# Moving low-part products, one tile offset and the start of the gathered rows in a two-layer fp32 transformer trunk

## The chip, the cores and the metric

One NeuronCore of one Trainium2 chip runs the whole program in one launch. The metric is device time in microseconds (us); lower is better. Each figure for a kernel is the median of several executions, and one execution was taken with the hardware profiler.

## The reference, cut to what matters

256 tokens of width 1024 go through two layers. Each layer is a mixer and a feed-forward part, each with a residual and a LayerNorm:

```python
for layer in range(2):
    mix = mla_mixer(h, ...) if layer == 0 else nsa_mixer(h, shared, ...)
    h = layer_norm(ALPHA * h + mix, ln_g[layer, 0], ln_b[layer, 0])
    ffn = peer_ffn(h, p_w_q[layer], p_subkeys[layer], p_u[layer], p_v[layer])
    h = layer_norm(ALPHA * h + ffn, ln_g[layer, 1], ln_b[layer, 1])
```

The feed-forward part picks 128 of 16384 experts for each token (8 heads, 16 each), and sums them with gates:

```python
u_e, v_e = u[experts], v[experts]
a = gelu(einsum("thkd,td->thk", u_e, xc))
out = einsum("thk,thkd->td", g * a, v_e)
```

All is float32.

## The kernel before, in words

**Split products.** Every weight block (128 partitions by 1024) is loaded by SyncE into a raw buffer, ScalarE casts it to a high part (`hi`, line 125, `_shi`), and VectorE subtracts to get the low part (`lo`, line 136, `_slo`). Activations are split in the same way: `hT[0]` holds the high part of the transposed hidden state and `hT[1]` the low part. A product is then three TensorE passes: high by high, low activation by high weight, high activation by low weight. Every product is issued at line 202. `hi` and `lo` have four buffers each. A high tile is allocated 32 elements longer than its contents, and `self.odd` says whether a tile begins at element 32 or 0 for every second buffer; a weight that is not in `self.odd` always begins at 0.

**Order.** Nothing reorders the program: each engine takes its instructions in the order in which the Python code issues them. `nxt()` hands out the next weight of one long list and prepares the two behind it (`prep`).

**Stages.** The order is mixer A, feed-forward 0, mixer B, feed-forward 1. A feed-forward stage does all experts instead of gathering for most tokens: (1) queries and scores, with VectorE's top-k work drained beside TensorE ("side" work); (2) the u stage, 128 steps `u_step`, one per block of 128 experts, which from the point where the routing is done works "wide" (512 columns at once, high by both parts of `hT`, then low by high); (3) the v stage, 128 steps `v_mm`, each with six products for token tile 0 and four for token tile 1. The last 64 tokens are not in the dense sums: for these VectorE adds 64 gathered tiles of `p_v` rows, one row for each partition (`g_mac`, line 493), GpSimd gathers the rows (`g_row`, line 479, a ring of `RING = 6`) and the activations that belong to them out of a DRAM scratch `actD` (`g_act`, line 483, four columns per small tile `gel`, multiplied into the gates at line 488). `actD` is written from the u stage (line 770). Row `gc` is added at the step `j` at which `j >= LEAD + int(rate * gc)` with `rate = (P - 8 - LEAD) / 64`. The low part of the next weight stands ahead of the row in VectorE's order. In the last steps weights are held in "keep" tiles so that token tile 1 can be finished behind token tile 0.

**Joints.** Between two stages the LayerNorm stands on the path: sum (line 273, or 854 and 855), statistics (276), `ln_mid` (285 to 292), `ln_center` (280) and `ln_scale` (298), then `ln_T`: four transposes on TensorE (229), a copy by ScalarE (312, high part) and a subtraction by VectorE (313, low part), which `ln_T` returns as a function to be issued later. Token tile 0 is normalised first; the work of tile 1 then runs beside early products of the next stage (`early_mm(tt, x, w, tiles)`: token tile, part of the activation, part of the weight, and which of four weights). Each such entry is a pair of products, 24 entries in all; `early_mm` leaves out those that were done, and `early_close` does the rest. `lo_aside` has GpSimd make the first low weight. Joint A leads from mixer A to feed-forward 0 and joint C from mixer B to feed-forward 1 (both through `out_close`); joint B leads from feed-forward 0 to mixer B (end of `peer`). The end of feed-forward 1 has no next stage and no transposes.

Of the kernel before, what the change touches and what calls it, by code (L numbers as in the profile page):

```python
# [34 lines left out]
FIRST, NEXT = 44, 10  # L35
GT = 64
ND = S - GT
RING, LEAD = 6, 7
AHEAD = 12
GB = 0.8  # L40
GS = 2.0 ** 15
# [2 lines left out]
class Kern:  # L44
# [276 lines left out]
    def ln_last(self, early, los=()):  # L321


        los, done = list(los), bool(los)
        if early:
            self.early_open()
            self.early_mm(0, 0, 0, (0, 1))
            self.early_mm(0, 1, 0, (0, 1))
        if not done:
            los.append(self.ln_T(0, 1))  # L330
        if early:
            self.early_mm(0, 0, 0, (2, 3))
        for hf in range(2):
            self.ln_scale(1, hf)
            if done and hf == 0:
                los.pop(0)()
            los.append(self.ln_T(1, hf))
            if done and early and hf == 0:
                self.early_mm(0, 1, 0, (2, 3))
            if early and hf == 0:  # L340
                self.early_mm(1, 0, 0, (0, 1))
        for f in los:
            f()
# [105 lines left out]
    def peer(self, l):  # L449
        tc, nc, I = self.tc, self.nc, self.I  # L450
        self.v0 = self.v0s.pop(0)
        with ExitStack() as es:
# [188 lines left out]
            done = {"g": 0, "a": 0}  # L641

            def g_flush(n=1):
                if len(gq) < n:
                    return
                while gq:
                    t0, oi, gs = gq.popleft()
                    ps = self.acc(t0 // 4 % 2)
                    for q in range(4):
                        for w in range(2):  # L650
                            self.mm(ps[:, q * P:(q + 1) * P], oi[:, q // 2, :, q % 2], gs[w][:, q // 2, :, q % 2],
                                    w == 0, w == 1)
                    pv = ps.rearrange("p (t j) -> p j t", t=4)
                    k = done["a"]
                    for x, j0, n in A:
                        m = min(max(k, 0), n)
                        if m > 0:
                            y = x[:, 0:m, t0:t0 + 4]
                            nc.vector.scalar_tensor_tensor(y, pv[:, j0:j0 + m], 1.0 / GS, y, op0=OP.mult, op1=OP.mult)  # L659
                        if m < n:  # L660
                            nc.scalar.activation(x[:, m:n, t0:t0 + 4], pv[:, j0 + m:j0 + n], AF.Copy, scale=1.0 / GS)
                        k -= n
                    done["g"] = t0 + 4
# [63 lines left out]
            def u_step(j):  # L727
                hi, lo = self.nxt()
                ps = self.ps()
                wide = len(A) > 1  # L730
                if wide:

                    def high(k):
                        self.mm(ps, hi[:, k * P:(k + 1) * P], self.hTT[:, k].rearrange("p a t -> p (a t)"), k == 0, k == KC - 1)

                    for k in range(KC - 1):
                        high(k)
                    for k in range(KC):
                        self.mm(ps[:, 0:S], lo[:, k * P:(k + 1) * P], xhi[:, k, :], False, False)
                    high(KC - 1)  # L740
                else:
                    self.proj_T(ps[:, 0:S], hi, lo, xhi, xlo, KC)
                return j, ps, wide
# [4 lines left out]
            def u_fin(x):  # L748
                while due:
                    y, ps = due.popleft()  # L750
                    nc.vector.tensor_tensor(y, y, ps, op=OP.mult)
                if x is None:
                    return
                j, ps, wide = x
                jj = (P - FIRST + j) % P
                y, n = slot(jj), done["g"]
                if wide:
                    t = gat.tile([P, S], F32, tag="half", name="half", bufs=2)
                    nc.scalar.copy(t, ps[:, S:2 * S])  # L759
                    nc.vector.tensor_tensor(ps[:, 0:S], ps[:, 0:S], t, op=OP.add)  # L760
                if n:
                    nc.scalar.activation(ps[:, 0:n], ps[:, 0:n], AF.Gelu)  # L762
                    due.append((y[:, 0:n], ps[:, 0:n]))
                if n < ND:
                    nc.scalar.activation(y[:, n:ND], ps[:, n:ND], AF.Gelu)  # L765
                if j % 4 == 0:
                    gst.append(gat.tile([P, 4, GT], F32, tag="gst", name="gst", bufs=2))
                nc.scalar.activation(gst[-1][:, j % 4, :], ps[:, ND:S], AF.Gelu)  # L768
                if j % 4 == 3:
                    nc.gpsimd.dma_start(self.actD[:, jj - 3:jj + 1, :], gst.pop())  # L770
                done["a"] = j + 1
# [24 lines left out]
            for j in range(P):  # L796
                x = u_step(j)
                u_fin(pu)
                pu = x
                g_flush(2)  # L800
                run_side(1.6 if len(A) == 1 else GB)
                if not side and len(A) == 1:
                    es_r.close()
                    if l == 1:
                        self.odd.update((i, 0) for i in range(self.si, self.v0))
                    hot = self.pr8.tile([P, 2, 3, 2, P, 2], F16, tag="r8", name="hot")
                    A.append((self.pr8.tile([P, NEXT, ND], F32, tag="r8", name="A2"), 0, NEXT))
                    n = P - FIRST - NEXT
                    A.append((pool(es_1, "slots1").tile([P, n, ND], F32, name="A1"), NEXT, n))
                    side.append(g_gen(hot))  # L810
                if done["g"] == ND and j >= P - 3 and not W:
                    w_start()
# [36 lines left out]
            def sum_1(f):  # L849

                t = self.ps()
                c, z = accs[1][f], hN[0:P - GT, 1, f * 512:(f + 1) * 512]
                nc.scalar.copy(t[0:P - GT], c[P - GT:P])
                nc.vector.scalar_tensor_tensor(z, z, ALPHA, c[0:P - GT], op0=OP.mult, op1=OP.add)
                nc.vector.tensor_tensor(z, z, t[0:P - GT], op=OP.add)
# [36 lines left out]
            early = l == 0 and "nsa" in self.parts  # L892
# [12 lines left out]
            lo0 = []  # L905
            for f in range(2):
                for j in range(P - NT, P - 3):
                    v_mm(j, 1, (f,), False, j == P - 4)
                    if f == 1 and j == P - 7:
                        lo0.append(self.ln_T(0, 1))  # L910
                sum_1(f)
                if early and f == 0:
                    self.lo_aside()
                self.ln_stats(1, f)
                if f == 0:
                    self.ln_T(0, 0)()
            self.ln_mid(1)
            self.ln_last(early, lo0)
        return hN


# [230 lines left out]
    def out_close(self):  # L1152

        two, again = (0, 1), not self.oboth
        base = self.si + 2
        if again:
            self._slo(base + 1)
            self.oacc[1] = [self.acc(1) for _ in range(2)]
            self.out_mm(4, 1, two, True, False)
        self.out_step(6)  # L1160
        if again:
            self._slo(base + 2)
        self.warm(AF.Sqrt)
        self.out_step(7)
        self.ln_start(self.ohN, self.ogb, self.oacc)
        for hf in range(2):
            self.ln_sum(0, hf)
            self.ln_stats(0, hf)
        if again:
            self.out_mm(5, 1, two, False, False)  # L1170
        if again:
            self._slo(base + 3)
        self.ln_mid(0)
        if again:
            for k in range(4):
                self.owts[k] = self.nxt(False, False)
        early = "peer1" in self.parts if again else "peer0" in self.parts
        if early:
            self._shi(self.si + 3)
        for hf in range(2):  # L1180
            self.ln_scale(0, hf)

        for k in ((6, 7, 2, 3) if again else (5, 6, 7)):
            self.out_mm(k, 1, two, False, False)
        last = (0, 1) if again else (2, 3)
        for f in range(2):
            self.out_mm(last[0], 1, (f,), False, False)
            self.out_mm(last[1], 1, (f,), False, True)
            self.ln_sum(1, f)
            if early and f == 0:  # L1190
                self.lo_aside()
            self.ln_stats(1, f)
            if f == 0:
                self.ln_T(0, 0)()
        self.ln_mid(1)
        self.ln_last(early)

    def heads_T(self, dst, h0, ps):

# [475 lines left out]
```

## Time and profile before

| what | us |
|---|---|
| median of 3 runs | 1750.76 |
| lowest and highest of these | 1747.94, 1750.95 |
| the profiled execution, its own time | 1745.92 |
| span of its records | 1744.1 |

The profiled execution is one of its own, 4.84 us below the median. The 1.8 us between its time and its span lie outside the recorded instructions. Rows give times from the start of the span. A line of a timeline begins with start and length of a run of instructions in us, then engine, line, operation, output and inputs, and in brackets how long the engine had been idle before it and which engine and line ended that wait.

### The profile page before, as it was taken

Reading aid. Unit: us, or ns where it says so; the run is one execution under the profiler, and the core shown is the slowest. Engines: PE = TensorE matmul, PEld = TensorE weight load, DVE = VectorE, ACT = ScalarE, POOL = GpSimd, SP = SyncE. Lnnn points to the kernel's source line nnn. Section 1 sums busy time; section 2 is a strip of 40 time slices with the busy share of each in tenths; the row PEclk is TensorE's granted clock in tenths of the full one; section 3 lists DMA queues with packets and bytes.
Section 4 is the critical chain, followed back from the end, with each engine's and each line's share of the span. In section 5 each row is a group of like instructions: output and inputs, shape, how many; then the busy total and the mean of one; then the engine's idle time right before and its main releaser. Section 6 shows DMA issues by size and latency. Waiting matters only on the chain.

```text
span 1744.1 us, 30698 instructions
## 1 busy us (share of the span) xinstructions
PE 1702.4 (98%) x10610; PEld 1480.5 (85%) x10610; DVE 1553.4 (89%) x3667; ACT 1041.5 (60%) x2265; POOL 478.7 (27%) x441
## 2 busy tenths in 40 slices
PE   7999999999999999999998999999999999999997
PEld 6779999888888788888786789998888888888886
DVE  6778988989997899999767789988999998999998
ACT  6656555766666455556455755556666666555554
POOL 2010002000002777761342210002000005777740
PEclk9999999999999999999998999999999999999999
DMA  7545667555557799999572265657556558999992
GB/s 245 174 145 180 203 192 266 184 183 185 183 184 259 301 395 373 368 358 328 176 246 90 84 215 179 204 182 270 187 182 188 183 183 297 401 383 369 361 363 108
DMA packets 118619, 416.66 MB, mean 239 GB/s; under 512 B 16032, under 2 KB 18112, under 8 KB 117376
## 3 DMA queue, kind: packets, MB, share of 16 engines
q1 hardware_dynamic: 88976, 322.60, 54.6%
q0 software_dynamic: 29488, 92.10, 14.2%
q8 instruction: 84, 1.38, 0.3%
q14 instruction: 71, 0.58, 0.1%
HBM read 400.49 MB, written 13.63 MB: 237 GB/s over the span
## 4 chain that ended last, share of the span: by engine, by line
PE 69%; issue 16%; DVE 7%; DMA 3%; ACT 2%; POOL 2%; SPq 0%; POOLq 0%; ACTq 0%; DVEq 0%
PE acc L202 36%; PE mm L202 33%; DVE lo L136 2%; PE mm L229 1%; DMA actD<-gst 1%; POOL row L479 1%; POOL actD L770 1%; DVE keep L136 1%; DMA raw<-a_wv 1%; ACT hi L125 0%; DMA xT<-xT 0%; DMA gel<-actD,gidx 0%; POOL gel L483 0%; DVE gacc L493 0%; DVE W L786 0%
## 5 line engine op out<-in xcount | busy, mean ns | idle before, releaser
L125 ACT CAST hi<-raw 128x1024 fp32r<-128x1024 f32 (+1 forms) x463 | 484.3, 1048 | 237.8 <-PE acc L202 96.7
L202 PE MATMUL mm<-hT,hi 128*128 128x256 f32 (+1 forms) x3360 | 610.7, 328 | 0.0
L136 DVE TENSOR_TENSOR lo<-raw,hi 128x1024 fp32r<-128x1024 f32 (+1 forms) x459 | 559.3, 1222 | 29.2 <-ACT hi L125 27.7
L202 PEld LDWEIGHTS mm<-hT,hi 128*128 128x128 f32 x3360 | 484.0, 188 | 44.0 <-issue 1.2
L202 PE MATMUL acc<-hi,W 128*128 128x512 f32 x1452 | 408.7, 390 | 0.0
L202 PEld LDWEIGHTS acc<-hi,W 128*128 128x128 f32 x1452 | 273.2, 188 | 56.9
L202 PE MATMUL mm<-hT,lo 128*128 128x256 f32 x2376 | 320.0, 277 | 0.0
L202 PEld LDWEIGHTS mm<-hT,lo 128*128 128x128 f32 x2376 | 306.9, 188 | 15.1
L202 PE MATMUL acc<-lo,W 128*128 128x512 f32 x968 | 299.6, 391 | 2.6 <-DVE lo L136 2.6
L770 POOL DMA_DIRECT2D actD<-gst x64 | 34.8, 544 | 785.0 <-ACT gst L768 785.0
L479 POOL DMA_INDIRECT row<-p_v,gidx x128 | 195.4, 1527 | 119.0 <-DVE gacc L493 81.7
L202 PEld LDWEIGHTS acc<-lo,W 128*128 128x128 f32 x968 | 181.6, 188 | 42.1 <-DVE lo L136 4.9
L125 ACT CAST hi<-spare 128x1024 fp32r<-128x1024 f32 x122 | 128.1, 1050 | 115.9 <-PE acc L202 99.8
L483 POOL DMA_INDIRECT gel<-actD,gidx x128 | 162.8, 1272 | 49.9 <-issue 36.0
L493 DVE SCALAR_TENSOR_TENSOR gacc<-row,ggate,gacc 128x1024 f32<-128x1024 f32 x126 | 161.3, 1280 | 1.1
L136 DVE TENSOR_TENSOR lo<-spare,hi 128x1024 fp32r<-128x1024 f32 x122 | 148.8, 1219 | 5.8 <-ACT hi L125 5.1
L762 ACT ACTIVATE mm<-mm 128x192 f32<-128x192 f32 (+23 forms) x170 | 40.9, 241 | 122.6 <-DVE mm L760 122.6
L786 DVE TENSOR_TENSOR W<-A,W 128x128 fp32r<-128x128 f32 (+1 forms) x512 | 107.5, 252 | 1.8 <-ACT W L781 1.8
L760 DVE TENSOR_TENSOR mm<-mm,half 128x256 f32<-128x256 f32 x174 | 74.5, 428 | 15.5 <-ACT half L759 14.9
L781 ACT CAST W<-A 128x192 fp32r<-128x192 f32 x256 | 88.2, 346 | 0.0
L659 DVE SCALAR_TENSOR_TENSOR A<-acc,A 128x176 f32<-128x176 f32 (+16 forms) x268 | 56.8, 274 | 24.9 <-PE acc L202 19.9
L765 ACT ACTIVATE A<-mm 128x192 f32<-128x192 f32 (+23 forms) x244 | 67.4, 276 | 7.2 <-DVE mm L760 2.2
(276 smaller groups left out, 1755.6 us busy)
## 6 DMA issues: line engine op xcount, KB each, us to landing
raw<-p_u SPq DMA_DIRECT2D x256, 512.0 KB, 3.8
spare<-p_v SPq DMA_DIRECT2D x64, 1024.0 KB, 8.9
raw<-p_v SPq DMA_DIRECT2D x63, 1024.0 KB, 8.9
raw<-p_wq SPq DMA_DIRECT2D x32, 512.0 KB, 4.0
actD<-gst POOLq DMA_DIRECT2D x64, 128.0 KB, 3.8
raw<-b_wo SPq DMA_DIRECT2D x12, 512.0 KB, 3.5
raw<-a_wo SPq DMA_DIRECT2D x8, 512.0 KB, 4.2
raw<-s_wT SPq DMA_DIRECT2D x8, 512.0 KB, 4.3
```

The lines of the kernel that those rows point to most:

```text
L125: self.nc.scalar.copy(self.his[i], self.raws[i])
L136: e.tensor_tensor(self.los[i], raw, self.his[i].bitcast(F32), op=OP.subtract)
L202: self.nc.tensor.matmul(out, a, b, start=start, stop=stop)
L479: nc.gpsimd.indirect_dma_start(out=t, out_offset=None, in_=gtable, in_offset=bass.IndirectOffsetOnAxis(ap=gidx[:, 0, c:c + 1], axis=0))
L483: nc.gpsimd.indirect_dma_start(out=gel[c // 4][:, c % 4:c % 4 + 1], out_offset=None, in_=gplaces, in_offset=bass.IndirectOffsetOnAxis(ap=g ...
L493: nc.vector.scalar_tensor_tensor(gacc, t, gw[:, c:c + 1], gacc, op0=OP.mult, op1=OP.add)
L659: nc.vector.scalar_tensor_tensor(y, pv[:, j0:j0 + m], 1.0 / GS, y, op0=OP.mult, op1=OP.mult)
L760: nc.vector.tensor_tensor(ps[:, 0:S], ps[:, 0:S], t, op=OP.add)
L765: nc.scalar.activation(y[:, n:ND], ps[:, n:ND], AF.Gelu)
L770: nc.gpsimd.dma_start(self.actD[:, jj - 3:jj + 1, :], gst.pop())
L781: nc.scalar.copy(WW[j][:, 0:ND], slot(j))
L786: nc.vector.tensor_tensor(WW[j][:, o:o + c.stop - c.start], slot(j)[:, c], WW[j][:, c].bitcast(F32), op=OP.subtract)
```

## The change

Four edits. (1) `LEAD` goes from 7 to 11: the first gathered row is added at step 11 of the v stage, and the rest closer together; the last stays at step 118. (2) In both layers, and not in layer 1 alone, the high parts of u's weights begin at element 32 in every second buffer once the u stage is wide. (3) In joints A and C the low part of tile 0's first half is not subtracted right after its copy but after `ln_scale(1, 0)`, and the products that read it go behind tile 1's first transposes; in joint B the low part of tile 0's second half goes from behind `ln_scale(1, 0)` to ahead of `sum_1(1)`, and the products that read it ahead of tile 1's first transposes. (4) In all three joints two products with the first low weight (`early_mm(0, 0, 1, (0,))`) go from `early_close` to ahead of tile 1's first transposes.

```diff
-RING, LEAD = 6, 7
+RING, LEAD = 6, 11
...
     def ln_last(self, early, los=()):
-        los, done = list(los), bool(los)
+        los = list(los)
         if early:
             self.early_open()
             self.early_mm(0, 0, 0, (0, 1))
+        if los:
+            los.append(self.ln_T(0, 1))
+        elif early:
             self.early_mm(0, 1, 0, (0, 1))
-        if not done:
-            los.append(self.ln_T(0, 1))
         if early:
             self.early_mm(0, 0, 0, (2, 3))
+            if not los:
+                self.early_mm(0, 1, 0, (2, 3))
+            self.early_mm(0, 0, 1, (0,))
         for hf in range(2):
             self.ln_scale(1, hf)
-            if done and hf == 0:
+            if hf == 0 and los:
                 los.pop(0)()
             los.append(self.ln_T(1, hf))
-            if done and early and hf == 0:
-                self.early_mm(0, 1, 0, (2, 3))
             if early and hf == 0:
+                self.early_mm(0, 1, 0, (0, 1))
                 self.early_mm(1, 0, 0, (0, 1))
         for f in los:
             f()
...
                     es_r.close()
-                    if l == 1:
-                        self.odd.update((i, 0) for i in range(self.si, self.v0))
+
+                    self.odd.update((i, 0) for i in range(self.sh, self.v0))
...
                     if f == 1 and j == P - 7:
                         lo0.append(self.ln_T(0, 1))
+                for x in lo0:
+                    x()
                 sum_1(f)
...
             self.ln_mid(1)
-            self.ln_last(early, lo0)
+            self.ln_last(early)
...
             self.ln_stats(1, f)
             if f == 0:
-                self.ln_T(0, 0)()
+                lo0 = self.ln_T(0, 0)
         self.ln_mid(1)
-        self.ln_last(early)
+        self.ln_last(early, [lo0])
```

## Rows read from the trace of the kernel before

**Rows 1.** The page, part 1: TensorE's busy time, share and instructions.

```profile
PE 1702.4 (98%) x10610; PEld 1480.5 (85%) x10610; DVE 1553.4 (89%) x3667; ACT 1041.5 (60%) x2265; POOL 478.7 (27%) x441
```

**Rows 2.** Windows: stretch, length, busy per engine; wide u and v, each layer.

```profile
304.81:547.34 242.53, 242.53 (x1636) 212.49 (x1634) 223.02 (x553) 160.29 (x450) 10.80 (x20) 1.00 0.57 183
1200.79:1442.40 241.61, 241.61 (x1635) 212.50 (x1633) 223.67 (x555) 160.91 (x451) 10.80 (x20) 1.00 0.58 181
547.56:836.74 289.18, 286.37 (x1254) 235.73 (x1253) 273.09 (x469) 166.48 (x261) 175.93 (x126) 0.99 0.92 346
1442.63:1727.71 285.08, 284.86 (x1254) 234.59 (x1252) 272.72 (x469) 165.06 (x258) 171.29 (x126) 1.00 0.92 345
```

**Rows 3.** Timeline, TensorE, start of the v stage of layer 0.

```profile
570.27 0.61 PE L202 MATMUL acc<-hi,W 128*128 128x512 f32 x2
573.47 1.22 PE L202 MATMUL acc<-lo,W 128*128 128x512 f32 x2 [2.58 <-DVE lo L136]
...
576.89 0.62 PE L202 MATMUL acc<-hi,W 128*128 128x512 f32 x2
```

**Rows 4.** Chain of waits around that point: start, length, what.

```profile
564.54 6.63 DMA gel<-actD,gidx
```

**Rows 5.** Timeline, VectorE: the first gathered row of layers 0 and 1.

```profile
571.29 0.16 DVE L488 TENSOR_TENSOR ggate<-gel,ggate 128x4 f32<-128x4 f32 x1 [7.54 <-DMA gel<-actD,gidx]
...
1462.32 0.16 DVE L488 TENSOR_TENSOR ggate<-gel,ggate 128x4 f32<-128x4 f32 x1 [2.94 <-DMA gel<-actD,gidx]
```

**Rows 6.** Timeline, VectorE and TensorE, one step in mid v stage.

```profile
706.57 1.28 DVE L493 SCALAR_TENSOR_TENSOR gacc<-row,ggate,gacc 128x1024 f32<-128x1024 f32 x1
...
707.03 1.07 PE L202 MATMUL acc<-hi,W 128*128 128x512 f32 x4
...
707.76 1.22 DVE L136 TENSOR_TENSOR lo<-spare,hi 128x1024 fp32r<-128x1024 f32 x1
...
709.24 1.22 DVE L136 TENSOR_TENSOR lo<-raw,hi 128x1024 fp32r<-128x1024 f32 x1
709.30 1.07 PE L202 MATMUL acc<-hi,W 128*128 128x512 f32 x4
```

**Rows 7.** Windows of 1 us: PE, PEld, DVE, ACT, POOL busy, granted clock, DMA.

```profile
574.00:575.00 1.00, 1.00 (x4) 0.76 (x3) 1.00 (x2) 0.00 (x0) 0.70 (x2) 0.50 0.01 0
...
851.00:852.00 1.00, 1.00 (x3) 0.77 (x3) 1.00 (x2) 0.18 (x1) 0.63 (x2) 0.50 0.85 115
...
913.00:914.00 1.00, 0.00 (x0) 0.00 (x0) 0.62 (x2) 1.00 (x3) 0.00 (x0) 1.00 0.81 90
```

**Rows 8.** Timeline, joint A.

```profile
113.23 2.39 POOL L136 TENSOR_TENSOR lo<-raw,hi 128x1024 fp32r<-128x1024 f32 x1
...
113.67 0.67 DVE L313 TENSOR_TENSOR hT<-mm,hT 128x512 fp32r<-128x512 f32 x1
114.26 0.68 DVE L273 SCALAR_TENSOR_TENSOR hN<-hN,acc 128x512 f32<-128x512 f32 x1
...
118.40 0.63 PE L229 MATMUL mm<-ident,hN 128*128 128x128 f32 x4 [0.45 <-DVE hN L298]
...
122.00 2.59 PEld L202 LDWEIGHTS acc<-hi,hT 128*128 128x128 f32 x12 [0.19 <-ACT hT L312]
```

**Rows 9.** Timeline, joint B.

```profile
844.82 0.68 DVE L854 SCALAR_TENSOR_TENSOR hN<-hN,acc 64x512 f32<-64x512 f32 x1 [1.36 <-ACT mm L853]
...
849.45 0.68 DVE L313 TENSOR_TENSOR hT<-mm,hT 128x512 fp32r<-128x512 f32 x1
...
849.58 0.97 PE L229 MATMUL mm<-ident,hN 128*128 128x128 f32 x4 [2.64 <-DVE hN L298]
...
854.79 3.02 PE L202 MATMUL acc<-hi,hT 128*128 128x512 f32 x12 [0.68 <-ACT hT L312]
```

**Rows 10.** Timeline, joint C.

```profile
1008.53 1.64 PE L202 MATMUL acc<-keep,oT 128*128 128x512 f32 x6
...
1010.50 0.68 DVE L273 SCALAR_TENSOR_TENSOR hN<-hN,acc 128x512 f32<-128x512 f32 x1
```

## The prediction

> **What bounds the kernel now.** I read the page first: TensorE is busy for 98% of the span, VectorE for 89% [rows 1]. An edit that saves VectorE or GpSimd time is therefore worth only what TensorE waited for it, and the question for each edit is: at which place does TensorE stand still, or run slowly, on account of what is edited? Windows of 25 us over the whole span show full TensorE slices nearly everywhere, with dents at the start of layer 0's v stage, at the three joints and in mixer B's attention. Then I set the two feed-forward stages side by side, since they are one code on the same shapes: the wide u stage takes 242.53 us in layer 0 and 241.61 us in layer 1, the v stage (first product to the last run on keep tiles) 289.18 us and 285.08 us [rows 2]. Two of the edits touch just these differences. Last I read the timelines of the joints, engine by engine. The reader is to see in them who ends TensorE's waits: VectorE's scaling or ScalarE's copy, not a weight.
>
> **Edit 1, LEAD from 7 to 11.** In layer 0 TensorE breaks off after 570.27 and goes on at 573.47, released by a low part from VectorE [rows 3]. VectorE had stood for 7.54 us at the gates of the first gathered row [rows 5]; the chain shows what for, a gather of activations issued at 564.54 that takes 6.63 us to land [rows 4]. The low part of a later weight is queued behind that wait, so TensorE runs out of low weights. After the hole the granted clock is 0.50, the lower of its levels (1.2 against 2.4 GHz) [rows 7], and two products take 1.22 us; from 576.89 on they take 0.62 us again [rows 3]. The price is the difference of the v stages, 289.18 - 285.08 = 4.1 us [rows 2]: layer 1 waits too, 2.94 us [rows 5], but has no hole. A TensorE step is 709.30 - 707.03 = 2.27 us [rows 6]. Four steps more put the first row 4 x 2.27 = 9.1 us later, which exceeds 7.54 us by 1.5 us. What is late next: the same gather, if it should land more than 1.5 us later; and even then layer 1 shows that a wait of 2.94 us makes no hole. I take a gain of 4.1 us in layer 0 and nothing in layer 1; the bounds are 0 and 4.1.
>
> The cost of the edit is density. VectorE's step without a row is 709.24 - 707.76 = 1.48 us and a row adds 707.76 - 706.57 = 1.19 us [rows 6]. The rate was (128 - 8 - 7)/64 = 1.766 steps a row and becomes 1.703. So VectorE's mean step goes from 1.48 + 1.19/1.766 = 2.15 to 1.48 + 1.19/1.703 = 2.18 us; the gate products (0.16 us once in four rows [rows 5]) add 0.02 to both. TensorE's 2.27 us still covers it, by 0.07 us a step. If that cover were gone, each 0.01 us would cost 1.07 us in a layer's 107 steps. From step 113 on rows stand at the same steps as before (113 instead of 112 for one of them), so the end of the stage is left at its length; bounds 0 and 0.3 us of loss.
>
> **Edit 2, one offset for u's high parts in layer 0.** Layer 1 had it already, and its replacement of `si` by `sh` changes only tiles that are already made. The wide stretch does the same 80 steps in both layers, without a stall in either, and layer 1 is 0.92 us shorter [rows 2]. No instruction is added. I take 0.9 us of gain, bounds 0 and 0.9. The Trainium skill says in "SBUF — State Buffer", section "SBUF: two separate sides", that TensorE's SBUF port waits for nobody; by that rule an offset of a tile should change nothing, this term would be 0 and the sum 0.9 us smaller. The trace differs from it by those 0.92 us in two stretches of equal work, though it doesn't show that the offset is the reason.
>
> **Edits 3 and 4, joint A.** The low part of tile 0 stands in VectorE at 113.67, and the sum of tile 1's second half behind it at 114.26 [rows 8]; its products were done before. Without the low part the sum, the statistics and the whole of `ln_mid` come 0.59 us earlier, and so does `ln_scale(1, 0)`, which releases tile 1's transposes at 118.40 [rows 8]. The subtraction now stands between the two halves' scaling and delays the second half against the first by its 0.67 us [rows 8], so that this ends where it ended; TensorE has eight products between the two transposes now (the four that read the low part came there), 8 x 0.227 = 1.8 us at ten products a step of 2.27 us [rows 6], which cover it. Were they not there, the 0.59 us would be lost. Then two products with the first low weight move ahead of the transposes, where TensorE waited 0.45 us [rows 8]: 2 x 0.227 = 0.45 us, done in that wait and missing later. Their weight comes from GpSimd at 113.23 + 2.39 = 115.62 [rows 8], ahead of the first transposes by over 2 us, so no new wait. Sum for A: 0.6 + 0.45 = 1.05 us; bounds 0.45 and 1.1.
>
> **Joint C** is the same code. There VectorE's sum starts at 1010.50 though its products end at 1008.53 + 1.64 = 1010.17 [rows 10], so only 0.3 us is to be had from VectorE, and 0.45 us from the two products: 0.75 us, bounds 0 and 0.8.
>
> **Joint B.** VectorE's chain to tile 1's scaling isn't shortened: the low part of tile 0's second half goes to a place where VectorE stood for 1.36 us for ScalarE's copy [rows 9], so its 0.68 us cost nothing there (0.68 us if that wait were gone). The transposes still start at 849.58. But TensorE had waited 2.64 us for them [rows 9]; six products (four that read this low part and two of the first low weight), 6 x 0.227 = 1.36 us, now stand in this hole and 1.28 us is left. Behind the transposes the low part no longer stands ahead of the second half's scaling (849.45 [rows 9]), and only four products stand between the two transposes. In joint A the way from the first transposes to the products behind the second took 122.00 - 118.40 = 3.60 us [rows 8]; in B 854.79 - 849.58 = 5.21 us [rows 9], for the granted clock had fallen to 0.50 there [rows 7]. The question is whether it still falls. It fell after holes of 2.64 and 2.58 us [rows 3, 9], and it did not around 913, a microsecond without any TensorE work [rows 7]. With 1.28 us left I expect it not to fall: 5.21 - 3.60 = 1.6 us, and 0.45 us for the two products that are missing later, 2.05 us. If it falls, about what the slow stretch in layer 0 cost besides its hole is lost: 4.1 - 2.58 = 1.5 us. Bounds 0.5 and 2.1.
>
> **Sum.** 4.1 + 0.9 + 1.05 + 0.75 + 2.05 = 8.85 us. Everything behind a joint is TensorE work without a gap until the next dent, so the gains add up. Against the profiled execution: 1745.92 - 8.85 = 1737.1 us, a span of 1735.3. That execution is 4.84 us under the median of the runs shown, and the forecast is for such a median: 1750.76 - 8.85 = 1741.9 us. The runs shown lie 3 us apart, about 0.2%, which is also about what a measurement of this kernel can tell from no change.
>
> **Rivals.**
> (a) The clock still falls in joint B. For it: besides the 1.28 us there are two shorter waits for ScalarE's copies close behind (0.68 us before the last products [rows 9]). Against it: joint A has such short waits too (0.45 us, 0.19 us [rows 8]) and no slow clock. Gain 8.85 - 1.5 = 7.35 us: 1743.4. Chance 0.17.
> (b) The offset doesn't do it: the 0.92 us are due to something else in which the layers differ. Gain 7.95 us: 1742.8. Chance 0.10. The rule of the Trainium skill's page "SBUF — State Buffer" named above would have it so.
> (c) The gather lands late again. VectorE no longer stands still while GpSimd writes the next gathers, and weights keep streaming in, so the gather could take 6.63 us and several more. If the hole of layer 0 stays, edit 1 gives nothing: gain 4.75 us, 1746.0. Against it: layer 1's gather met steady streaming and its wait was 2.94 us [rows 5], less than the 9.1 us of delay. Chance 0.06.
> (d) The gain of joint B and of A behind it is given back in mixer B's attention, where TensorE has gaps anyway and its clock falls by the pattern of these gaps. Half of 8.85 us would be left: 1746.3. Chance 0.07.
> (e) Slower: VectorE becomes the bound of both v stages. Its step need only go from 2.20 to above 2.27 us, by rows of 1.30 instead of 1.19 us, or by waits for ScalarE between a low part and a row. From there each 0.01 us costs 2 x 1.07 = 2.1 us in the two layers; at 2.32 us the loss of 10.7 us exceeds all gains, at 2.35 us the kernel takes 1741.9 + 17.1 = 1759.0 us. For it: the cover is 3%. Against it: VectorE caught up after its wait of 7.54 us in layer 0 within the stage. Chance 0.04.
>
> **How the numbers follow.** The forecast as worked out has the remaining 0.56, and the time is its own: 1741.9 us. Its own range, by the bounds of A and C and the spread of the runs, is 1739.5 to 1744. The whole range goes from 1737.5 (the fast end of the runs shown, 1747.94 - 8.85 = 1739.1, and a further 1.6 us if gaps in the attention close) to 1746.5, which takes in (a) to (d) and leaves out (e). Faster by over 0.2% means under 1747.3: the forecast and (a) to (d), less what the spread of a median takes from (c) and (d): 0.88. Within 0.2%: 0.08. Slower: 0.04.
>
> **What the profile after would show.** Edit 1: no hole over 1 us and no clock of 0.50 in layer 0's first 30 us of the v stage, a wait at line 488 well under 2 us, and v stages of equal length. Edit 2: wide u stretches equal within 0.2 us. A: tile 1's first transposes about 0.6 us earlier against the sum of tile 1's first half, eight products behind them. B: a wait of about 1.3 us ahead of the transposes with a granted clock of 1.00, and 3.6 us from there to the products behind the second transposes. C: 0.3 us. The prediction is wrong if VectorE has no idle time left in the middle of the v stage while TensorE waits for line 136, or if line 488 still waits for its gather with a hole on TensorE.

## The result, and the profile after

| us | before | after | ratio, 95% interval |
|---|---|---|---|
| medians, first comparison (4 and 4 runs) | 1749.76 | 1737.44 | 0.9934 [0.9916, 0.9951] |
| medians, second comparison, taken later (13 and 8 runs) | 1747.5 | 1738.62 | 0.9953 [0.9936, 0.9970] |
| profiled execution, its time and span | 1745.92, 1744.1 | 1733.25, 1731.5 | |

Faster, as forecast. The forecast time of 1741.9 us was 4.5 us too high, and 1737.44 lies 0.06 us below the range; the forecast gain of 8.85 us is 3.5 us below the gain of the first comparison, 12.3 us, and equals that of the second, 8.9 us.

By stages, from the two profiled executions (lengths between the same instructions of either kernel):

| stage | before | after | gain | forecast |
|---|---|---|---|---|
| v stage of layer 0 | 289.18 | 284.82 | 4.4 | 4.1 |
| wide u of layer 0, behind the first one-hot products | 242.75 | 241.83 | 0.9 | 0.9 |
| joint A, first sum to first query product | 22.86 | 21.96 | 0.9 | 1.05 |
| joint B, first keep product to mixer B's first product | 24.59 | 22.55 | 2.0 | 2.05 |
| joint C, last six keep products to first query product | 16.24 | 15.65 | 0.6 | 0.75 |
| mixer B | 147.21 | 144.52 | 2.7 | 0 |
| all other stages | | | 1.2 | 0 |

The five terms sum to 8.8 us of a span shorter by 12.7. Read only so far, every step came true. The repeated profiles below show which of it was this execution's chance.

Windows of the changed kernel (stretch, length, busy per engine, granted clock, DMA share, GB/s): wide u of both layers, then v of both, answering to [rows 2].

```profile
302.92:544.54 241.62, 241.62 (x1636) 212.60 (x1634) 222.55 (x553) 159.97 (x450) 10.80 (x20) 1.00 0.58 184
1187.93:1429.54 241.61, 241.61 (x1636) 212.60 (x1633) 223.75 (x555) 160.90 (x451) 10.81 (x20) 1.00 0.57 181
544.76:829.57 284.81, 284.58 (x1253) 234.70 (x1252) 274.15 (x470) 167.44 (x261) 172.63 (x126) 1.00 0.94 351
1429.76:1715.02 285.26, 284.89 (x1254) 234.64 (x1252) 273.37 (x468) 165.41 (x258) 169.73 (x126) 1.00 0.92 345
```

The two u stretches are equal now, and the v stages differ by 0.45 us. VectorE's timeline at the first gathered row of the two layers has no bracket at the gates any more (line 491 here, line 488 before), where [rows 5] has waits of 7.54 and 2.94 us:

```profile
569.80 0.16 DVE L491 TENSOR_TENSOR ggate<-gel,ggate 128x4 f32<-128x4 f32 x1
...
1455.21 0.16 DVE L491 TENSOR_TENSOR ggate<-gel,ggate 128x4 f32<-128x4 f32 x1
```

TensorE's timeline in joint A of the changed kernel, answering to [rows 8]: the wait of 0.45 us ahead of the transposes at 117.68 is filled by the two low products, and eight products stand behind them. The last two lines are of the kernel before, for the same place.

```profile
116.05 1.19 PE L202 MATMUL acc<-hi,hT 128*128 128x512 f32 x4 [1.26 <-ACT hT L312]
117.07 0.63 PE L202 MATMUL acc<-lo,hT 128*128 128x512 f32 x2
117.68 0.63 PE L229 MATMUL mm<-ident,hN 128*128 128x128 f32 x4
118.19 2.12 PE L202 MATMUL acc<-hi,hT 128*128 128x512 f32 x8
120.14 0.60 PE L229 MATMUL mm<-ident,hN 128*128 128x128 f32 x4
...
119.70 1.19 PE L202 MATMUL acc<-hi,hT 128*128 128x512 f32 x4 [0.68 <-ACT hT L312]
120.73 0.60 PE L229 MATMUL mm<-ident,hN 128*128 128x128 f32 x4
```

Joint B, answering to [rows 9], with the window of 1 us behind it: a wait of 1.28 instead of 2.64 us, a granted clock of 1.00, and 846.05 - 842.42 = 3.63 us from the first transposes to the products behind the second (forecast 3.6).

```profile
840.52 0.62 PE L202 MATMUL acc<-lo,hT 128*128 128x512 f32 x2
842.42 0.66 PE L229 MATMUL mm<-ident,hN 128*128 128x128 f32 x4 [1.28 <-DVE hN L298]
...
846.05 3.02 PE L202 MATMUL acc<-hi,hT 128*128 128x512 f32 x12 [0.67 <-ACT hT L312]
...
849.00:850.00 1.00, 1.00 (x6) 0.83 (x5) 1.00 (x1) 0.00 (x0) 0.00 (x0) 1.00 1.01 426
```

### The profile page after: what moved, and what is told of

It reads as the page before. It is cut to its first block, busy times and chain, and to the rows that moved or that the text cites. A ratio compares the mean times of both kernels' runs of the same rounds, so it can differ in the third digit from the quotient of the medians.

```text
span 1731.5 us, 30701 instructions
## 1 busy us (share of the span) xinstructions
PE 1693.7 (98%) x10610; PEld 1474.7 (85%) x10610; DVE 1554.4 (90%) x3667; ACT 1041.6 (60%) x2265; POOL 474.2 (27%) x441
## 4 chain that ended last, share of the span: by engine, by line
PE 90%; DVE 5%; ACT 2%; DMA 1%; issue 1%; SPq 0%; POOL 0%; ACTq 0%; DVEq 0%
PE mm L202 50%; PE acc L202 39%; PE mm L229 1%; DVE keep L136 1%; DVE lo L136 1%; DMA xT<-xT 0%; DMA bounce<-ropeO 0%; DVE gacc L496 0%; ACT hi L125 0%; DVE W L789 0%; DVE qs L1377 0%; DMA spare<-p_v 0%; DVE bnst L276 0%; DVE m L1554 0%; ACT p L1561 0%
## 5 line engine op out<-in xcount | busy, mean ns | idle before, releaser
L482 POOL DMA_INDIRECT row<-p_v,gidx x128 | 191.1, 1493 | 122.9 <-DVE gacc L496 87.3
L662 DVE SCALAR_TENSOR_TENSOR A<-acc,A 128x176 f32<-128x176 f32 (+16 forms) x268 | 56.8, 274 | 24.4 <-PE acc L202 18.7
```

Source lines behind the costliest of these rows:

```text
L482: nc.gpsimd.indirect_dma_start(out=t, out_offset=None, in_=gtable, in_offset=bass.IndirectOffsetOnAxis(ap=gidx[:, 0, c:c + 1], axis=0))
```

## The experiments

Theory: the five terms add, each at its own place. Rivals: the offset does nothing; joint B's clock is no matter of the shortened wait; VectorE has no cover left. "Step 7" and "step 11" are the values of LEAD.

**One part at a time.** Four kernels: step 11 alone, the offset alone, the joints' edits alone, and the kernel before once more.

```diff
 x1_lead, on before:       -RING, LEAD = 6, 7     +RING, LEAD = 6, 11
 x2_offset, on before:     -if l == 1: self.odd.update((i, 0) for i in range(self.si, self.v0))
                           +self.odd.update((i, 0) for i in range(self.sh, self.v0))
 x3_joints, on after:      both of these undone
 x4_before_again:          nothing
```

> The kernel before with LEAD at 11 and nothing else. Theory (the hole in layer 0's v stage is the whole price of LEAD): v stage of layer 0 falls from 289.18 to about 284.9 us, that of layer 1 stays at 285.1, no wait over 2 us at the gates, all other stages as before, 4.3 us in all. Rival (the late gather is kept late by the streaming weights): the hole stays and v stays near 289. For the 0.66 and 0.44 us that TensorE waited for the one-hot tiles at the start of the wide u stage: if they went because of the joints, they are still here.

> The kernel before with the offset of u's high parts in both layers and nothing else. Theory (the offset makes the 0.92 us): wide u stretch of layer 0 at 241.61 instead of 242.53 us, layer 1 unchanged at 241.61, everything else as before. Rival (something else in which the layers differ): 242.53 stays.

> The changed kernel with LEAD back at 7 and the offset back as it was: only the edits of the joints. Theory (the parts add up): joint A 22.0, B 22.6, C 15.7 us (before 22.9, 24.6, 16.2), the granted clock in B at 1.00, layer 0's v stage back at 289 us with its hole; if the joints also made VectorE early for the one-hot tiles, the waits of 0.66 and 0.44 us there are gone here and only here; if not, they are back. Rival (the joints' gain hangs on the earlier v stage): B near 24.

> The kernel before, unchanged, once more. Theory (2.7 us of the difference between the two profiles lie in mixer B's attention and are a matter of the execution, not of the change): mixer B differs here from its 147.2 us by a microsecond or more, or the run lies by as much off 1745.9, while the other stages repeat within 0.2 us. Rival (the change shortened it): mixer B repeats at 147.2 within 0.3 us.

Measured: step 11 alone 1742.45 against 1746.38 us, ratio 0.9976 [0.9953, 1.0000]; the joints alone 1743.45, 0.9981 [0.9956, 1.0006]; one run each of the offset, 1746.07, and of before, 1746.01. By these intervals neither part alone is clear of no change. With step 11, layer 0's v stage is 284.81 us and the gates wait for nothing. With step 7 it differs from profile to profile: 289.18, 286.43, 288.97 and 286.91 us, with holes of TensorE of 2.74, 1.07, 2.37 and 1.08 us (counted from where the next product was due, some 0.16 us more than the bracket of a row); the clock fell behind the two longer ones only. Windows of that v stage, in step 11 alone:

```profile
548.28:833.09 284.81, 284.58 (x1253) 234.67 (x1252) 273.40 (x470) 167.14 (x261) 176.32 (x126) 1.00 0.94 351
```

The kernel before once more: wide u and v stage of layer 0, then layer 1's v stage.

```profile
304.94:547.47 242.53, 242.53 (x1636) 212.62 (x1633) 222.97 (x553) 160.30 (x450) 10.81 (x20) 1.00 0.55 183
...
547.69:834.12 286.43, 285.20 (x1253) 234.61 (x1252) 272.20 (x470) 165.45 (x261) 182.81 (x126) 1.00 0.93 349
1438.51:1727.79 289.28, 287.60 (x1254) 235.58 (x1252) 272.79 (x469) 165.25 (x258) 176.06 (x126) 0.99 0.91 340
```

Here the long v stage is layer 1's (289.28 against 285.08 in [rows 2]): behind a gate wait of 2.84 us a gap of 0.87 us came 40 us into the stage, and the clock fell behind it. So the difference of the two layers on which the first term was built is itself partly an execution's. In the offset's stretch nothing varies: 242.75 us in every profile of layer 0 without the offset, 241.83 or 241.84 with it (but once 241.94, and once 243.41 with a slow clock in the stretch). The joints A and C repeat to 0.05 us: 22.86 and 16.04 to 16.08 without the edits (but once 16.24, in the profile that the prediction read), 21.93 and 15.66 with them. Mixer B took 147.43 us in the kernel before once more, which is what the rival had expected; that it varies by the execution shows in 145.55 us with step 11 alone and 148.38 us with the offset alone.

Joint B went against the theory. The kernel before kept its clock this time, behind the same wait of 2.64 us, and the joint took 23.19 us:

```profile
846.97 0.65 PE L229 MATMUL mm<-ident,hN 128*128 128x128 f32 x4 [2.64 <-DVE hN L298]
...
851.00:852.00 1.00, 1.00 (x5) 0.82 (x5) 1.00 (x2) 0.00 (x0) 0.00 (x0) 1.00 1.00 426
```

and the joints' edits, with the wait of 1.28 us, lost it, for 6.8 us, and took 25.42 us. The rival of that run, that the joints' gain hangs on the earlier v stage, had expected a slow joint B:

```profile
846.95 0.66 PE L229 MATMUL mm<-ident,hN 128*128 128x128 f32 x4 [1.28 <-DVE hN L298]
...
849.00:850.00 1.00, 1.00 (x5) 0.70 (x4) 0.00 (x0) 0.00 (x0) 0.00 (x0) 0.50 0.80 156
```

**The changed kernel again, the other offset, no low products, a late start.**

```diff
 y1_after_again:    nothing
 y2_other_offset:   -self.odd.update((i, 0) for i in range(self.sh, self.v0))
                    +if l == 0: self.odd.update((i, 1) for i in range(self.sh, self.v0))
 y3_no_first_low:   -self.early_mm(0, 0, 1, (0,))
 y4_lead30:         -RING, LEAD = 6, 11     +RING, LEAD = 6, 30
```

> The changed kernel, unchanged, once more, and timed beside the kernel before. If the 12.7 us between the two profiles are the change's alone, the median is 11 to 13 us below that of before, joint B takes 22.5 to 22.6 us with the clock at 1.00 and mixer B 144.5 us again. If, as the six profiles so far suggest, part of it is the executions' own chance (the clock in joint B, 1.4 to 1.8 us; in mixer B, up to 3 us; the wait for the first one-hot products, up to 1.5 us), then only these are fixed here: joint A 21.9 to 22.0, wide u's plain steps 2.75 in both layers, layer 0's v stage 284.8 without a hole, joint C 15.7; joint B is 22.5 to 22.6 where the clock stays up and about 24 to 25.4 where it falls; and the median is 7 to 9 us below before (hole 2 to 4, offset 1.1, joint A 0.9, joint B 0.6, joint C 0.5, first one-hot wait 0 to 1.5).

y1: the second comparison of the table, 8.9 us between medians. The fixed stages came back (v 284.78, joint A 21.93, B 22.55, C 15.62, the offset's stretch 241.84); mixer B took 146.64 us, so 2.1 of the 2.7 us that it had seemed to gain were chance.

> The changed kernel, but in layer 0's wide u the other one of the two tiles of high parts has the offset, and in layer 1 neither has. Theory (the place itself is slower, whichever step it is): layer 0's plain steps are all at 2.77 us, so about 84 x 0.0133 = 1.1 us more than the kernel before and 2.2 more than the changed one; layer 1's go 2.75 and 2.77 in turn, 1.1 us more than the changed kernel. Rival 1 (what is slow is that the two tiles stand alike): layer 0 all at 2.75, layer 1 in turn. Rival 2 (the offset does nothing and something else differs between the runs): both layers at 2.75.

y2: the theory that the place itself is slower. In layer 0 all plain wide steps (without one-hot products) are at 2.77 us; the stretch is 0.9 us longer than before's and 1.8 longer than the changed kernel's, where the theory had 1.1 and 2.2. Layer 1, without an offset, has before's length of layer 0. Windows of both:

```profile
303.63:547.07 243.44, 243.44 (x1636) 212.46 (x1634) 222.89 (x554) 160.80 (x450) 10.82 (x20) 1.00 0.55 182
1193.73:1436.26 242.53, 242.53 (x1636) 212.49 (x1634) 223.57 (x555) 161.31 (x452) 10.82 (x20) 1.00 0.55 181
```

> The changed kernel without the two products of tile 1's first low part that stand ahead of tile 1's transposes in all three joints. Theory: each joint gets its 0.45 us back as a wait of TensorE: joint A 22.4 (22.0 with them), joint C 16.1 (15.65), and in joint B the hole ahead of the transposes is 1.7 us instead of 1.28 and the stage 0.45 us longer at an equal clock. Rival (the joints' gain is the order of the transposes alone; the two products only fill a hole that is bounded by VectorE's chain, and the same two products done later fit in a later hole): the joints are within 0.1 us of the changed kernel's.

y3: joint A 22.39, joint C 16.07, joint B 23.00 us: 0.43 to 0.46 us in each, the theory's. The two products left out are of token tile 0, by `early_mm`'s first argument, and not of tile 1, as the expectation says; the same holds for the next low weight in z1 below. Without them TensorE waits for VectorE's scaling ahead of tile 1's transposes again, by 0.43 us in joint A and 0.45 us in joint C, although a longer wait for ScalarE's copy (1.25 and 1.18 us) stands ahead of that:

```profile
117.38 0.63 PE L229 MATMUL mm<-ident,hN 128*128 128x128 f32 x4 [0.43 <-DVE hN L298]
...
1008.89 0.63 PE L229 MATMUL mm<-ident,hN 128*128 128x128 f32 x4 [0.45 <-DVE hN L298]
```

In joint C the two products are the whole gain. The transposes come 5.83 us behind the start of the last keep products, where they came at 6.11 us in the profile that the prediction read, but at 5.91 or 5.92 us in the four others without the edits. In the kernel before once more, for one, VectorE's sum starts at 1006.53, only 0.15 us behind the end of its products at 1004.74 + 1.64 = 1006.38:

```profile
1004.74 1.64 PE L202 MATMUL acc<-keep,oT 128*128 128x512 f32 x6
...
1006.53 0.68 DVE L273 SCALAR_TENSOR_TENSOR hN<-hN,acc 128x512 f32<-128x512 f32 x1
```

In joint B the clock stayed at 1.00 behind a wait longer than that of the joints alone:

```profile
844.47 0.66 PE L229 MATMUL mm<-ident,hN 128*128 128x128 f32 x4 [1.72 <-DVE hN L298]
...
850.00:851.00 1.00, 1.00 (x6) 0.79 (x6) 1.00 (x2) 0.89 (x1) 0.00 (x0) 1.00 1.00 410
```

> The changed kernel with the gathered rows' work begun at step 30 instead of 11. The 64 rows then have to be worked off in 90 steps (1.41 steps for a row instead of 1.83). Theory of rival e of the forecast (VectorE becomes the bound of the v stages): VectorE's step is then 1.475 + 1.20/1.406 + 0.03 = 2.36 us against TensorE's 2.265, so each v stage gets 90 x 0.09 = 8 us longer less the lead that VectorE has, some 4 to 8 us, 290 us in both layers. Other theory (the row work's spare time is larger than that, since the low parts may run late by two steps and more): both stages stay within 1 us of 284.8. The wait of the first gate is nothing by both.

y4: 1767.07 us; the v stages take 301.78 and 297.13 us, 17 and 12 us longer, more than either theory gave. (The changed kernel has 1.70 steps for a row, not 1.83.) The same 50 us in this kernel and in the changed one:

```profile
750.00:800.00 50.00, 47.67 (x201) 36.75 (x200) 46.84 (x79) 25.73 (x40) 33.53 (x29) 1.00 0.96 362
```

```profile
750.00:800.00 50.00, 50.00 (x222) 41.45 (x221) 49.28 (x83) 28.65 (x44) 25.26 (x18) 1.00 0.98 364
```

VectorE, which should bound, is not even full (46.84 of 50). The groups of VectorE over layer 0's v stage of this kernel show what it waits for:

```profile
L136 DVE TENSOR_TENSOR lo<-spare,hi 128x1024 fp32r<-128x1024 f32 x61 | 74.3, 1218 | 8.6 <-ACT hi L125 8.6
L136 DVE TENSOR_TENSOR lo<-raw,hi 128x1024 fp32r<-128x1024 f32 x59 | 71.9, 1218 | 15.9 <-ACT hi L125 8.7 <-issue 5.9 <-remote 1.3
```

24.5 us of waits, 17.3 of them for ScalarE's high parts (7.5 and 5.8 in the changed kernel). The likely loop, argued from the order of the instructions and not tested: TensorE, waiting for low parts, frees the high tiles late, ScalarE fills them late, and VectorE waits for these on top of its own work. Rival (e)'s step length gives the point where the cover ends, not the price behind it. Joint B took 25.34 us in this kernel: behind a wait of 1.27 us the clock fell.

```profile
859.73 0.66 PE L229 MATMUL mm<-ident,hN 128*128 128x128 f32 x4 [1.27 <-DVE hN L298]
...
862.00:863.00 1.00, 1.00 (x5) 0.80 (x4) 0.00 (x0) 0.00 (x0) 0.00 (x0) 0.50 0.75 147
```

**A candidate, a smaller step, and the sum without the joints.**

```diff
 z1_second_low, on after: in peer, behind lo_aside():  +self._slo(self.si + 1, nc.gpsimd)
                          -self.early_mm(0, 0, 1, (0,))   +self.early_mm(0, 0, 1, (0,) if los else (0, 1))
 z2_lead9, on after:      -RING, LEAD = 6, 11    +RING, LEAD = 6, 9
 z3_no_joints:            before with step 11 and the offset
 z4_joints_again:         as the joints alone
```

> A candidate for a faster version: the changed kernel, and in joint B GpSimd also makes the mixer's second low weight, right behind the first (2.4 us, 837.6 to 840.0 in the changed kernel's time), and its two products with tile 1's high parts follow those of the first ahead of tile 1's transposes. Theory: they fill 0.45 us of the 1.28 us that TensorE waits there for VectorE's scale, so the wait is 0.83 us and joint B 22.55 becomes 22.1, where the clock stays up; GpSimd's transfers for mixer B start 2.4 us later, which costs nothing if they are wanted later than 10 us on. Rival 1: GpSimd's second subtraction slows VectorE's chain beside it (its 0.7 us instructions between 837.6 and 840.0) and the scale comes later by as much as is won, joint B 22.5 to 23. Rival 2: the loads that now start 2.4 us later hold up mixer B, up to 2.4 us. Between medians, 0.5 us can't be told from no change: ratio to the kernel before 0.993 to 0.996.

z1: joint B 22.09 us, the theory's 22.1; the wait is 0.81 us. Median 1738.01 against 1744.85 us, ratio 0.9956 [0.9942, 0.9970]: faster than the kernel before, and not to be told from the changed one (0.9953).

```profile
842.16 1.08 PE L202 MATMUL acc<-lo,hT 128*128 128x512 f32 x4
844.06 0.66 PE L229 MATMUL mm<-ident,hN 128*128 128x128 f32 x4 [0.81 <-DVE hN L298]
```

> The changed kernel with the gathered rows' work begun at step 9 instead of 11. The gates then stand in VectorE's queue at about V0+20.5 us. In the kernel before and in the joints-only kernel (step 7) the gather had landed at V0+22.1 to 23.7, a wait of 6.0 to 7.5 us cost a hole of 1.07 to 2.74, so some 4.9 us of it were free. Theory (the hole is what the wait exceeds VectorE's lead by): a wait of 2 to 4 us in layer 0, 0 to 1 in layer 1, no hole of TensorE over 0.5 us, v stages 284.8 and 285.2. Rival (any wait costs, since the row ring has to catch up later, as in the 1.1 us gap that one run of the kernel before shows at V1+39 after a wait of 2.8 us): a gap of about 1 us some 35 to 45 us into layer 0's stage and 285.5 to 289 us.

z2: a wait of 3.53 us at the gates in layer 0, none in layer 1, no hole, v stages 284.90 and 285.19: a wait below some 4.9 us makes no hole at that place (with step 7, wait less hole is 4.8 to 5.0 us in each profile). The rival's later gap came in one stage of the six with a wait of 2.8 to 3.6 us, layer 1 of the kernel before once more. In joint B the clock fell behind a wait of 1.27 us (25.40 us).

```profile
572.76 0.16 DVE L491 TENSOR_TENSOR ggate<-gel,ggate 128x4 f32<-128x4 f32 x1 [3.53 <-DMA gel<-actD,gidx]
```

> The kernel before with the later start of the gathered rows and with the offset, but none of the joints' edits. If the parts add: joint A 22.86, joint C 16.05, joint B 23.2 with the clock at 1.00 and 24.6 to 24.8 where it falls, wide u of layer 0 253.8 to 254 and layer 0's v stage 284.8; the median 4 to 6 us below the kernel before (hole 2 to 4, offset 1.1, part of the wait for the first one-hot products). If the joints' edits carry most of the gain instead, only 1 to 3 us below. On joint B's clock: with the joints' edits it stayed up in four of five looks where VectorE was in time, without them in one of four; a fall here would be one more for the edits, a clock of 1.00 one more for chance.

z3: 1741.01 against 1744.85 us, ratio 0.9976 [0.9967, 0.9985], 2.6 to 5.8 us. Joint A 22.87, C 16.08, the v stage 284.80, the offset's stretch 241.84: the parts add stage by stage. The 3.8 us between the medians lie between what the two theories gave, 4 to 6 and 1 to 3 us, and decide nothing. In joint B the clock fell (24.78 us).

> The joints' edits alone once more (step 7, old offset), for joint B's clock. Theory that the fall there is the execution's chance and not the wait's length: the wait ahead of the transposes is 1.28 us again, and the stage is 22.5 us if the clock stays up or 23.9 to 25.4 if it falls, either of them possible. Rival, that something ahead of the joint which the two other edits remove makes it fall (the hole in layer 0's v stage): it falls again. Layer 0's v stage has a hole again, 1.0 to 2.8 us, joint A 21.9, joint C 15.65.

z4: the hole in the v stage is 1.13 us, the clock stays up behind it, and it falls again in joint B (25.36 us), as the rival had it. The hole itself is not what makes it fall, since it also fell in z2, which has none; but what else step 11 changes is not excluded.

## Why the prediction was right, and where only its sum was

**Step 11: right mechanism, size off.** The wait, the hole and its disappearance are as forecast, also that layer 1 gains nothing (285.08 to 285.61 us with step 7 outside the one long stage, 285.04 to 285.26 with step 11). But 4.1 us was one execution's price. Five profiles with step 7 give 286.4 to 289.2 us, 287.6 in the mean, against 284.8: the term is 2.8 us. What it left out is the spread. On one chip, 19 runs of the kernel before lie between 1741.6 and 1754.6 us and the joints alone between 1737.9 and 1752.6, but step 11 alone between 1739.7 and 1745.8. On the chip of z1 to z4, though, the 15 runs of the kernel before lie within 4.9 us. The chance gap in layer 1 seen above is one candidate for what disappears; no run isolates it.

**The density's price was nothing,** as forecast: 284.8 us with rows every 1.70 steps. Step 30 shows that the cover does end, and that more than the longer step has to be paid there.

**The offset: right,** 0.91 us against 0.9, and now shown to be the offset: the stretch is 243.66, 242.75 or 241.84 us as all, half or none of the tiles have the slow place. The rule cited from the Trainium skill ("SBUF — State Buffer", section "SBUF: two separate sides"), that TensorE's port waits for nobody, would have made it 0; the measurement decides against that use of it.

**Joint A: 0.91 for 1.05.** The two low products gave their 0.46, and tile 1's transposes did come 0.6 us earlier against the first sum. But 0.13 us of that were lost behind them: from these transposes to the second ones it is 120.14 - 117.68 = 2.46 us with eight products and 120.73 - 118.40 = 2.33 us before, with a wait and four products. The step "8 x 0.227 = 1.8 us" is 1.95 us by the rows (120.14 - 118.19). The longer wait for ScalarE's copy ahead of the transposes (1.26 us, 0.74 before) cost nothing, as y3 shows: behind it TensorE still had to wait for VectorE. **Joint C: 0.41 for 0.75,** all of it from the two products. The step that failed is "0.3 us is to be had from VectorE": it was read from the one profile in which VectorE's sum came late. Against the four others the transposes come only 0.09 us earlier, and the 0.13 us behind them take that back.

**Joint B: the step that failed is "with 1.28 us left I expect it not to fall".** The profiled pair agreed with it to 0.01 us, and the clock did not fall in the second profile of the change either. But the wait's length is not the reason, by all fourteen profiles:

| joint B | wait, us | first row at step | joint B, us | clock |
|---|---|---|---|---|
| before; before again; offset alone | 2.64 | 7 | 24.59; 23.19; 24.79 | fell; stayed; fell |
| step 11 alone; no joints (z3) | 2.65; 2.64 | 11 | 24.58; 24.78 | fell in both |
| joints alone, twice (x3, z4) | 1.28 | 7 | 25.42; 25.36 | fell in both |
| step 9 (z2) | 1.27 | 9 | 25.40 | fell |
| step 30 (y4) | 1.27 | 30 | 25.34 | fell |
| after; after again; other offset | 1.28; 1.27; 1.28 | 11 | 22.55; 22.55; 22.56 | stayed in all |
| no low products (y3) | 1.72 | 11 | 23.00 | stayed |
| second low weight (z1) | 0.81 | 11 | 22.09 | stayed |

Behind a wait of 1.27 or 1.28 us the clock fell in four profiles of seven, though TensorE's rows of these seven agree to 0.02 us from the first keep product to the four products behind the transposes. Sorted by the step, it stayed up in all five with the joints' edits and step 11 and fell in all four with these edits and another step, and each of two chips saw both outcomes. Only the kernel before shows both outcomes in one kernel. So two accounts are open: a lot that each execution draws, or something that the start of the gathered rows changes ahead of the joint. The split was seen only after the runs, no run was made to tell the two apart, and further profiles of the changed kernel and of the joints alone would. At a clock of 1.00 the edits are worth 23.19 - 22.55 = 0.64 us; with a fallen clock the joint is 0.6 us longer with them (25.4) than without (24.6 to 24.8).

The trace of the kernel before already spoke against the step. It names 913, where the clock held behind a wait of 1.32 us; but a little later in mixer B the clock was at 0.50 behind a wait of 1.12 us and one of 0.41 us:

```profile
922.80 0.39 PE L202 MATMUL mm<-ks,qs 128*128 128x256 f32 x1 [1.12 <-ACT p L1553]
...
923.71 0.50 PE L202 MATMUL acc<-ks,qs 128*128 128x512 f32 x1 [0.41 <-ACT p L1556]
...
925.00:926.00 1.00, 1.00 (x7) 1.00 (x6) 0.99 (x2) 0.00 (x0) 0.92 (x1) 0.50 0.50 111
```

The Trainium skill ("TensorE: Matmul & The Clock Gate", section "Part 1: The HAM clock gate (the "warmup" mystery)") says that the number of slow products at the start of one and the same kernel varies from run to run. The two profiles of the kernel before agree with that, in the middle of a kernel.

**The sum.** What repeats is 2.8 + 0.9 + 0.9 + 0.6 + 0.4 = 5.6 us with joint B at a clock of 1.00 on both sides, and 6.8 us if joint B is counted at the mean of the five profiles without the edits (24.4 us) and the 22.55 us of the changed kernel, against 8.85 forecast and 5.2 to 11.2 us by the second comparison's interval (8.6 to 14.7 by the first). The parts' own medians, 0.24% for step 11 and the offset and 0.19% for the joints (with an interval that takes in no change), sum to 7.5 us and fit the second. The 2 to 3 us beyond 5.6 are not traced to a place: joint B's clock is one candidate, and mixer B (144.5 to 148.4 us over all profiles, with no pattern by kernel) and the wait for the first one-hot products of layer 0's wide u (0 to 1.9 us) vary by about as much or more from profile to profile.

Rivals: (b) is excluded and so is (c); (e) has its mechanism but the change stays clear of it; (a), that the clock still falls in joint B, came true in neither profile of the change, and at the same wait with other steps in all four; (d), which had the gain given back in mixer B, cannot be told from that stage's own spread.

## What to carry to other kernels

Before an execution's hole or slow clock is priced, look at the same stage in a second profile of the same kernel: two stages of one trace that differ by 4 us may owe it to chance, while what repeats to 0.01 us (here the offset) can be believed at 0.9 us. Before an outcome that differs between profiles is called chance, sort the profiles by each edit, as for the clock in joint B. When products are moved into a wait, count their time against the wait: between tile 1's transposes in joints A and C, eight products took 0.13 us more than a wait and four products had. Filling a known wait with products that are owed anyway paid its exact length in all four places tried (0.42 to 0.46 us each).

## What the runs showed of the hardware

The buffers of u's high parts start in turn at a slower and a faster place: a wide step of TensorE takes 2.77 us from the one and 2.75 us from the other, and moving a tile by 128 bytes turns the one into the other, each way.

GpSimd's gathers of activations in layer 0, the fourth and fifth, took 0.95 us each to issue while VectorE stood at the gates (joints alone) and 1.82 to 1.97 us while it worked on low parts (the kernels with step 11). The Trainium skill ("SBUF — State Buffer", section "SBUF: two separate sides") says that a VectorE instruction with two inputs in SBUF and a GpSimd instruction that reads SBUF exclude each other; a low part is such a subtraction, and a gather reads its places from the tile `gidx`. The trace agrees with that only in part: from the first gathered row on VectorE does these subtractions too, and the gathers take 1.03 to 1.17 us (from 570.67 on in the changed kernel), so the cause is not shown. Here it cost nothing: the fourth was out at 18.8 instead of 17.9 us into the stage, ahead of the gates at 25.0.
